# Twenty-three instead of twenty-one MLP pairs in block products, weights rounded by DMA, and a new planned order

## The chip, the cores and the metric

The kernel runs on 1 core of one Trainium2 chip. The metric is the device time of one execution in microseconds (us), lower is better. The inputs are float32, one batch of 256 tokens with 1024 features.

## The reference

Two decoder layers. Each has a token mixer (block-sparse attention in layer 0, dilated window attention in layer 1) and then an MLP; each half ends in a layer norm. What the change touches is the MLP, with `x` of 256 x 1024, `w_in` of 1024 x 4096 and `w_out` of 4096 x 1024:

```python
def sq_relu_mlp(x, w_in, w_out):
    return jnp.square(jax.nn.relu(x @ w_in)) @ w_out

for i in range(2):
    mix = moba_attention(h, ...) if i == 0 else dilated_attention(h, ...)
    h = layer_norm(ALPHA * h + mix, ...)
    h = layer_norm(ALPHA * h + sq_relu_mlp(h, w_in[i], w_out[i]), ...)
```

## The kernel before, in words

**Products in three terms.** A float32 operand is split into a high part, rounded to the matmul type `fp32r` (tile `whi` for weights), and a low part, the rest (`wlo`). A product is the sum of hi*hi, hi*lo and lo*hi, so one float32 product costs three matmuls on TensorE (PE). A weight tile is 128 x 1024, 512 KB. It is loaded by SP into a `raw` buffer (7 of them, `NRAW`), ScalarE (ACT) writes `whi` (10 buffers), and VectorE (DVE) subtracts and writes `wlo` (10 buffers); this is `split` (L406 to L414) called by `load_near`.

**The far path.** For the tiles named in `FAR` and `FAR_W`, DVE is spared: `far_parts` (L422) lets ACT write `whi` (L423) and minus `whi` into `wlo` (L424), and then GpSimd (POOL) issues a DMA that reads the weight tile from HBM a second time and adds it into `wlo` (L425). `FAR` names MLP tiles, one set for each layer: `("f", p, t)` is tile t of pair p in the first product, `("o", p, k)` and `("s", p, n)` are tiles of the second. `FAR_W` numbers the 58 other tiles (projections, and the head of each MLP) in program order.

**Pairs.** The 4096 hidden columns are 16 pairs p of 256. For pairs 2 to 15 the first product is `do_first` (L1207), a step `fpt` for each half t: 8 matmuls of 512 columns and 8 of 256. `half_sum` (L1124) then adds two halves of the PSUM bank, by an ACT copy and a DVE addition, and `square` (L1130) makes the squared ReLU, by two ACT instructions where `SQUARES` says `A`, by one DVE instruction where it says `D`. Pairs 0 and 1 come from `head` and `half` (L1158, L1164).

**Ordinary pairs and block products.** The second product of a pair is ordinary (`o` or `O`, `do_out`, L1236) or a block product (`a` or `A`, `do_duo`, L1249). An ordinary pair multiplies two weight tiles for two halves of the tokens: 24 matmuls of 512 columns. A block product treats pair and weights as 2 x 2 blocks and needs seven products instead of eight: 21 matmuls of 512 columns, 9 in its step `a`/`A` and 12 in its step `b`. For that DVE and ACT make more: `duo_sums` (L660) forms sums of the activation blocks (four subtractions or additions of 128 columns, and low parts of 512 and 384 columns), and `load_duo` (L677) loads two raw tiles, forms four sums of 512 columns of weights (two before the first step, two before the second) and splits half a tile and three whole ones. Where a pair is in `BY_DMA`, the first two of the four sums are made by one adding DMA from POOL (L698). `combine` (step `z`, L1281) adds the seven products up into the output tokens. Upper-case letters make the activation parts early, in cells of their own that `Cells` hands out, lower-case ones when needed.

**The order.** `STEPS` (L37) is the order of the work on PE in each MLP, written out: first products, block products and ordinary pairs are mixed so that weights and sums come in time. `Plan` (L145 on) holds every operation with a cost; `Plan.order` works out due times backwards from PE's order, lists every engine's operations in a simulated order, and emits them so; each engine then runs its list in order. `landed` (L113) is the planner's cost of a transfer. `GB_AT` and `MASK_AT` name the steps at which the layer-norm weights and the second attention mask are loaded. Around the step lists stand the attention stages and the layer norms, which the change does not reorder by hand.

**The end.** After `z` the last ordinary pairs run, for tokens 0 to 127 and then 128 to 255 (`out_and_ln`, L1090), while DVE does `combine` and the first layer norm; then comes the last layer norm (`ln_last`, L1022).

Of the kernel before, what the change touches and what calls it, by code (L numbers as in the profile page):

```python
# [347 lines left out]
def tile_trunk(  # L348
# [94 lines left out]
    def load_near(src, n=1024):
        w = W()
        w.raw = mk([P, 1024], F32, "raw", NRAW)
        w.hi = mk([P, 1024], F32R, "whi", NHI)
# [1 line left out]
        dma(lambda: w.raw.t[:, :n], src[:, :n], (), [(w.raw, 0)], P * n * 4)
        split(
            n, lambda: w.raw.t[:, :n], lambda: w.hi.t[:, :n], lambda: w.lo.t[:, :n],  # L450
            [(w.raw, 0)], [(w.hi, 0)], [(w.lo, 0)], sbuf=True,
        )
        return w

# [1173 lines left out]
```

## Time and profile before

| | |
|---|---|
| time, median of 3 runs | 546.07 us (546.03 to 546.39) |
| time of the profiled execution | 548.12 us |
| its span, first to last instruction | 546.3 us |
| mean granted TensorE clock | 0.996 |
| DMA from POOL (queue q0) | 37 issues, 19.40 MB |
| loads from HBM by SP (queue q1) | 104.35 MB |
| mean DMA rate | 229 GB/s |

The profile is one execution. Busy time of an engine is the time in which one of its instructions runs; instructions overlap a little, so the pitch from one start to the next is what an instruction really takes of a busy engine. Matmul ends are modelled, so PE is read by the starts too. In a row such as `L413 DVE TENSOR_TENSOR wlo<-raw,whi`, L413 is the line (here of a helper), `wlo<-raw,whi` what is written from what. A bracket `[1.06 <-DVE q0lo L749]` says how long the engine stood idle before, and what released it. Rows of the view by stretches hold, for each engine, its busy time and instructions, then the granted clock, the share of the 16 DMA engines and GB/s.

### The profile page before, as it was taken

What the parts mean: (1) busy time and instruction counts of PE and PEld (TensorE: products, weight loads), DVE (VectorE), ACT (ScalarE), POOL (GpSimd) and SP (SyncE); (2) the same over time, 40 slices, a digit from 0 to 9 for tenths busy, and PEclk for the clock granted to TensorE, in tenths of its full rate; (3) what the DMA queues carried; (4) which work ended last, traced back from release to release, by engine and by line L of the source; (5) the groups of instructions that cost most, each with busy time, mean ns of one, the idle gap of its engine ahead of it and who ended that gap; (6) DMA issues with size and microseconds to landing.
All of it is one profiled execution on the core that took longest, in us unless ns stands there. A gap on an engine that the chain in (4) does not pass through costs nothing.

```text
span 546.3 us, 8734 instructions
## 1 busy us (share of the span) xinstructions
PE 537.5 (98%) x3172; PEld 458.5 (84%) x3172; DVE 476.1 (87%) x846; ACT 389.8 (71%) x613; POOL 41.7 (8%) x52
## 2 busy tenths in 40 slices
PE   9999999999999999999999999999999999999994
PEld 7989888888888878888888889888888888888884
DVE  6679998897899899899857789879889899899997
ACT  6558999278799768798645558746876997877530
POOL 0000010010001000100011000110010100100001
PEclk9999999999999999999999999999999999999998
DMA  8987787929869879979998756865894989885602
GB/s 331 343 328 242 190 196 197 382 88 308 229 155 237 279 220 288 225 182 324 338 252 224 253 179 173 246 201 138 277 278 118 227 280 268 261 202 178 215 24 78
DMA packets 35611, 125.03 MB, mean 229 GB/s; under 512 B 3952, under 2 KB 4848, under 8 KB 35568
## 3 DMA queue, kind: packets, MB, share of 16 engines
q1 hardware_dynamic: 29664, 104.35, 55.9%
q0 software_dynamic: 5328, 19.40, 19.7%
q10 hardware_dynamic: 576, 0.72, 0.4%
q8 instruction: 25, 0.41, 0.3%
q14 instruction: 18, 0.15, 0.1%
HBM read 123.40 MB, written 1.05 MB: 228 GB/s over the span
## 4 chain that ended last, share of the span: by engine, by line
PE 94%; DVE 2%; DMA 2%; ACT 0%; issue 0%; POOL 0%; DVEq 0%; POOLq 0%; ACTq 0%
PE acc L417 59%; PE tp L417 32%; PE tp L890 3%; DMA raw<-in_win_dram 2%; DVE wlo L413 1%; ACT whi L408 0%; DVE raw L749 0%; POOL rstd L1004 0%; DVE tok L756 0%; DVEq L1622 0%; DVE ta L749 0%; DVE ta L413 0%; DVE pt L413 0%; DVE bst L1035 0%; ACT ta L1127 0%
## 5 line engine op out<-in xcount | busy, mean ns | idle before, releaser
L413 DVE TENSOR_TENSOR wlo<-raw,whi 128x1024 fp32r<-128x1024 f32 (+2 forms) x200 | 222.8, 1137 | 22.1 <-ACT whi L408 20.2
L408 ACT ACTIVATE whi<-raw 128x1024 fp32r<-128x1024 f32 (+2 forms) x198 | 191.0, 995 | 49.8 <-PE acc L417 14.4
L417 PE MATMUL acc<-xs,whi 128*128 128x512 f32 (+1 forms) x496 | 113.4, 374 | 1.1 <-DVE q0lo L749 1.1
L417 PEld LDWEIGHTS acc<-xs,whi 128*128 128x128 f32 x496 | 87.1, 191 | 17.8 <-DVE q0lo L749 1.5
L417 PEld LDWEIGHTS acc<-xs,wlo 128*128 128x128 f32 x448 | 60.0, 191 | 3.5 <-issue 0.2
L417 PE MATMUL acc<-xs,wlo 128*128 128x256 f32 x448 | 62.5, 283 | 0.0
L417 PE MATMUL tp<-xs,whi 128*128 128x512 f32 x224 | 56.3, 392 | 0.0
L417 PE MATMUL acc<-whi,ahi 128*128 128x512 f32 (+1 forms) x130 | 49.7, 392 | 0.0
L417 PEld LDWEIGHTS tp<-xs,whi 128*128 128x128 f32 x224 | 40.4, 189 | 7.3
L417 PE MATMUL acc<-wlo,ahi 128*128 128x512 f32 (+1 forms) x109 | 42.3, 388 | 0.0
L423 ACT ACTIVATE whi<-raw 128x1024 fp32r<-128x1024 f32 x28 | 29.5, 1053 | 16.4 <-PE acc L417 15.3
L417 PE MATMUL acc<-whi,alo 128*128 128x512 f32 (+1 forms) x108 | 39.3, 388 | 0.0
L417 PEld LDWEIGHTS tp<-xs,wlo 128*128 128x128 f32 x224 | 30.5, 190 | 2.1
L417 PE MATMUL tp<-xs,wlo 128*128 128x256 f32 x224 | 31.5, 283 | 0.0
L424 ACT ACTIVATE wlo<-whi 128x1024 fp32r<-128x1024 f32 x28 | 29.6, 1058 | 0.4
L417 PE MATMUL acc<-whi,xs 128*128 128x512 f32 (+1 forms) x112 | 29.0, 364 | 0.0
L417 PEld LDWEIGHTS acc<-whi,ahi 128*128 128x128 f32 x130 | 24.4, 188 | 5.0 <-issue 0.3
L749 DVE TENSOR_TENSOR ta<-acc,ta 128x256 f32<-128x256 f32 x41 | 17.0, 421 | 12.1 <-ACT ta L777 8.7
L417 PE MATMUL tp<-whi,xs 128*128 128x512 f32 x80 | 25.4, 396 | 0.0
L417 PE MATMUL acc<-whi,ta 128*128 128x512 f32 (+1 forms) x72 | 24.5, 384 | 0.0
L417 PEld LDWEIGHTS acc<-whi,alo 128*128 128x128 f32 x108 | 20.3, 188 | 4.2
L417 PEld LDWEIGHTS acc<-wlo,ahi 128*128 128x128 f32 x109 | 20.5, 188 | 3.8
(246 smaller groups left out, 947.8 us busy)
## 6 DMA issues: line engine op xcount, KB each, us to landing
raw<-in_win_dram SPq DMA_DIRECT2D x64, 512.0 KB, 5.7
raw<-in_wout_dram SPq DMA_DIRECT2D x64, 512.0 KB, 6.1
raw<-in_wqk_dram SPq DMA_DIRECT2D x22, 512.0 KB, 8.9
raw<-in_wo_dram SPq DMA_DIRECT2D x14, 512.0 KB, 5.3
wlo<-in_win_dram POOLq DMA_DIRECT2D x10, 512.0 KB, 9.2
raw<-in_wout_dram POOLq DMA_DIRECT2D x9, 512.0 KB, 8.5
raw<-in_wv_dram SPq DMA_DIRECT2D x8, 512.0 KB, 5.4
wlo<-in_wqk_dram POOLq DMA_DIRECT2D x7, 512.0 KB, 9.2
```

The costliest lines, as they stand in the source:

```text
L408: op("ACT", act(n, sbuf=sbuf), lambda: nc.scalar.activation(hi(), src(), AF.Copy), r, whi)
L413: lambda: nc.vector.tensor_tensor(lo(), src(), f32(hi()), op=ALU.subtract), list(r) + list(whi), wlo,
L417: nc.tensor.matmul(out_ap, lhsT, rhs, start=start, stop=stop)
L423: op("ACT", act(1024, sbuf=True), lambda: nc.scalar.activation(hi.t, raw.t, AF.Copy), keys, [(hi, 0)])
L424: op("ACT", act(1024, sbuf=True), lambda: nc.scalar.activation(lo.t, f32(hi.t), AF.Copy, scale=-1.0), [(hi, 0)], [(lo, 0)])
L749: op("DVE", dve(n) + extra, lambda: nc.vector.tensor_tensor(out_ap(), a(), b(), op=alu), r, w)
L890: nc.tensor.transpose(ps.t[:, c : c + P], src(), ident.t)
```

## The change

- `STEPS` is new. Layer 0 has 11 block products and 5 ordinary pairs instead of 10 and 6, layer 1 has 12 and 4 instead of 11 and 5. As before, 2 ordinary pairs of layer 0 and 3 of layer 1 come after `z`.
- `M` is a new kind of block product: its activation parts lie in the buffer of the attention mask (`m1`) while that is free. (`G`, the same in the buffers of the layer-norm weights, and the undivided first chunk, `whole`, are in the code and not used by these lists.) The mask for layer 1 is loaded at step `b9` instead of `f21`, the layer-norm weights at `fb1` instead of `fc1`.
- `CAST` and `CAST_W` name 12, 11 and 21 tiles, 44 in all, whose `whi` is written by a DMA from POOL that rounds on the way from HBM (`cast_in`), instead of by ACT. Where the tile is not `FAR` as well, SP still loads the raw tile for DVE's low part; where it is both, no raw tile is loaded.
- `FAR` and `FAR_W` name 11, 13 and 7 tiles (31) instead of 8, 6 and 14 (28). 15 of the 31 are also rounded by DMA. Three of them, `("s", 5, 1)`, `("s", 5, 2)` and `("s", 10, 2)`, are weight sums: the adding DMA reads them from their buffer and not from HBM.
- `BY_DMA` keeps one pair of nine (pair 6 of layer 1). `TWICE` would make the second two sums by DMA too, but only for pairs in `BY_DMA`, and it does not name pair 6 of layer 1; so that branch is not taken.
- `SQUARES` gives 3 pairs of layer 0 and 4 of layer 1 to DVE.
- The planner takes buffers of a tag in turn instead of the one free first, and has new costs for a DMA that adds (8.8 instead of 8.4) or rounds (7.0).

The diff, cut to its core:

```diff
 STEPS = (
-    "f20 fd0 f21 f30 fc0 f40 f31 f41 fa0 fd1 f80 fa1 f90 A4 f50 f81 f51 Aa Ad fc1 ba f70 bd b4 A2 fb0 f91 "
-    "b2 ac fe0 f71 fe1 A3 f60 bc ff0 f61 b3 ff1 Ae fb1 A6 a7 be b6 A8 o1 b7 b8 ob o0 o9 z O5 Of",
-    "f20 f21 fd0 f30 fc0 f40 fd1 f41 fa0 f80 f31 f81 f50 fa1 f51 Ad f90 Aa A4 fc1 ba f70 b4 f71 bd A2 b2 "
-    "f91 ac fe0 fe1 fb0 f60 A3 bc ff0 b3 ff1 f61 A5 fb1 Ae a7 b5 be A6 O9 o1 b7 Ab b6 bb z Of o0 o8",
+    "f30 fc0 f31 fc1 f50 fa0 fa1 f80 f81 f20 f51 f40 A3 f21 fd0 fe0 b3 M2 fb0 fb1 f41 fd1 b2 A8 f90 b8 "
+    "fe1 Ac f91 f70 ff0 ff1 Ab f60 f61 bc bb A9 A5 f71 b9 b5 Aa ba a4 b4 Af O6 a7 b7 bf oe o0 z o1 Od",
+    "fd0 f40 f80 fd1 fc0 f81 f41 f50 f30 f51 fc1 A4 f70 f71 fb0 fb1 f31 A8 fe0 Ac fa0 b4 bc fe1 f20 f90 "
+    "A3 fa1 b3 b8 Ad f21 Mb f91 bd Aa bb ff0 ff1 ba f60 f61 A7 b7 Af o1 bf A5 a6 M2 b5 b2 b6 z Oe o0 O9",
 )
-BY_DMA = ({2, 6, 8, 14}, {2, 5, 6, 10, 14})
+BY_DMA = (set(), {6})
 FAR = (
-    {("f", 7, 0), ("f", 10, 1), ("f", 12, 0), ("f", 12, 1), ("f", 14, 1), ("o", 1, 1), ("s", 6, 0), ("s", 10, 0)},
-    {("f", 2, 1), ("f", 7, 0), ("f", 11, 0), ("f", 14, 1), ("s", 10, 0), ("s", 14, 0)},
+    {("f", 2, 1), ("f", 4, 0), ("f", 6, 0), ("f", 11, 1), ("f", 13, 1), ("f", 15, 1), ("o", 1, 0), ("s", 5, 1), ("s", 5, 2), ("s", 7, 0), ("s", 9, 0)},
+    {("f", 2, 0), ("f", 3, 1), ("f", 10, 0), ("f", 13, 0), ("f", 13, 1), ("f", 14, 0), ("o", 1, 0), ("o", 1, 1), ("s", 6, 0), ("s", 8, 0), ("s", 10, 0), ("s", 10, 2), ("s", 11, 0)},
 )
-FAR_W = {0, 12, 14, 16, 21, 32, 34, 35, 36, 39, 43, 48, 53, 57}
-GB_AT, MASK_AT = "fc1", "f21"
-SQUARES = ("AAAAAAAAAAAAAAAA", "AAAAAAAAAAAAAAAA")
+FAR_W = {10, 26, 34, 42, 51, 53, 56}
+GB_AT, MASK_AT = "fb1", "b9"
+CAST = (
+    {("f", 2, 1), ("f", 3, 0), ("f", 3, 1), ("f", 4, 0), ("f", 4, 1), ("f", 12, 0), ("f", 13, 1), ("o", 0, 1), ("o", 1, 0), ("o", 13, 0), ("o", 14, 1), ("s", 15, 0)},
+    {("f", 2, 0), ("f", 4, 0), ("f", 8, 0), ("f", 10, 0), ("f", 13, 0), ("f", 13, 1), ("f", 14, 0), ("o", 0, 1), ("o", 1, 0), ("o", 1, 1), ("s", 11, 0)},
+)
+CAST_W = {0, 4, 7, 10, 11, 15, 16, 18, 19, 21, 22, 29, 36, 38, 39, 43, 45, 50, 51, 53, 54}
+TWICE = ({2, 3, 9, 10, 11, 12, 15}, {8, 10, 11, 12, 13})
+SQUARES = ("AAAAADAAAAAADAAD", "AAAADDAAAADAAADA")
 def kinds_of(i):
-    at = {int(x[1], 16): x[0] for x in STEPS[i].split() if x[0] in "oOaA"}
-    return ["sS"["aA".index(at[p])] if at[p] in "aA" else at[p] for p in range(DFF // 256)]
+    at = {int(x[1], 16): x[0] for x in STEPS[i].split() if x[0] in "oOaAGM"}
+    return [at[p].replace("a", "s").replace("A", "S") for p in range(DFF // 256)]
...
         bus = max(t + DMA_FETCH, bus) + o.xfer / 370e3
-        return bus, max(bus, t + DMA_LANDS)
+        return bus, max(bus, t + (DMA_CASTS if o.xfer % 2 else DMA_LANDS))
     t = max(t + FETCH, bus)
     t += o.xfer / next(rate for until, rate in RATES if t < until)
...
-                s = max(s, sorted(slots[tag])[len(bs) - 1])
+                s = max([s] + slots[tag][: len(bs)])
...
                 if not b.held:
-                    slots[b.tag].remove(min(slots[b.tag]))
...
-DMA_ISSUE, DMA_FETCH, DMA_LANDS, DMA_RING = 1.0, 2.0, 8.4, 6
+DMA_ISSUE, DMA_FETCH, DMA_LANDS, DMA_CASTS, DMA_RING = 1.0, 2.0, 8.8, 7.0, 6
...
-    def far_parts(raw, hi, lo, src, keys):
-        op("ACT", act(1024, sbuf=True), lambda: nc.scalar.activation(hi.t, raw.t, AF.Copy), keys, [(hi, 0)])
+    def cast_in(hi, src):
+        op("POOL", DMA_ISSUE, lambda: nc.gpsimd.dma_start(hi.t, src), (), [(hi, 0)], xfer=P * 1024 * 4 - 1)
+    def add_in(lo, hi, src, keys=()):
         op("ACT", act(1024, sbuf=True), lambda: nc.scalar.activation(lo.t, f32(hi.t), AF.Copy, scale=-1.0), [(hi, 0)], [(lo, 0)])
-        op("POOL", DMA_ISSUE, lambda: nc.gpsimd.dma_start(lo.t, src, accum_op=ALU.add), (), [(lo, 0)], xfer=P * 1024 * 8)
-    def load_far(src):
+        op("POOL", DMA_ISSUE, lambda: nc.gpsimd.dma_start(lo.t, src(), accum_op=ALU.add), keys, [(lo, 0)], xfer=P * 1024 * 8)
+    loads = [0]
+    def load_w(src):
+        loads[0] += 1
+        return load_as(src, loads[0] - 1 in FAR_W, loads[0] - 1 in CAST_W)
+    def load_as(src, far, cast):
         w = W()
-        w.raw = mk([P, 1024], F32, "raw", NRAW)
+        if not (far and cast):
+            w.raw = mk([P, 1024], F32, "raw", NRAW)
         w.hi = mk([P, 1024], F32R, "whi", NHI)
         w.lo = mk([P, 1024], F32R, "wlo", NLO)
-        dma(lambda: w.raw.t, src, (), [(w.raw, 0)], P * 1024 * 4)
-        far_parts(w.raw, w.hi, w.lo, src, [(w.raw, 0)])
+        if not (far and cast):
+            dma(lambda: w.raw.t, src, (), [(w.raw, 0)], P * 1024 * 4)
+        if cast:
+            cast_in(w.hi, src)
+        else:
+            op("ACT", act(1024, sbuf=True), lambda: nc.scalar.activation(w.hi.t, w.raw.t, AF.Copy), [(w.raw, 0)], [(w.hi, 0)])
+        if far:
+            add_in(w.lo, w.hi, lambda: src)
+        else:
+            low_part(w.raw, w.hi, w.lo, [(w.raw, 0)])
         return w
...
+        def spot(self, tag):
+            if tag in self.gone:
+                raise ValueError(tag)
+            b = mk([P, 1024], F32R, tag, 1)
+            return [(b, 0, 0), (b, 512, 1)]
...
-        def wide(t, src=None):
+        def wide(t, part, src, again):
             h, l = [mk([P, 1024], F32R, tag, n) for tag, n in (("whi", NHI), ("wlo", NLO))]
-            if src is not None:
-                far_parts(t, h, l, src, [(t, 0), (t, 1)])
-                return [(h, l, c, 0) for c in (0, 512)]
-            split(1024, lambda: t.t, lambda: h.t, lambda: l.t, [(t, 0), (t, 1)], [(h, 0)], [(l, 0)], sbuf=True)
+            keys = [(t, 0), (t, 1)]
+            if part in cast:
+                cast_in(h, src)
+            else:
+                op("ACT", act(1024, sbuf=True), lambda: nc.scalar.activation(h.t, t.t, AF.Copy), keys, [(h, 0)])
+            if part in far:
+                add_in(l, h, again, [] if src is not None else keys)
+            else:
+                low_part(t, h, l, keys)
             return [(h, l, c, 0) for c in (0, 512)]
         split(512, x0, part(hi, q * 512, 512), part(lo, q * 512, 512), xk[:1], [(hi, q)], [(lo, q)], sbuf=True)
-        w3, w2 = wide(y, pair[:, 1024:] if far else None)
+        w3, w2 = wide(y, 0, pair[:, 1024:], lambda: pair[:, 1024:])
         if by_dma:
             op(
                 "POOL", DMA_ISSUE, lambda: nc.gpsimd.dma_start(x.t, pair[:, 512:1536], accum_op=ALU.add), xk, xk,
             tt(512, x0, x0, x1, ALU.add, xk, xk[:1])
             tt(512, x1, x1, y0, ALU.add, xk[1:] + yk[:1], xk[1:])
         yield w2, w3, (hi, lo, q * 512, q)
-        w5, w7 = wide(x)
-        tt(512, y0, y0, x0, ALU.add, yk[:1] + xk[:1], yk[:1])
-        tt(512, y1, y1, y0, ALU.add, yk, yk[1:])
-        w6, w4 = wide(y)
+        w5, w7 = wide(x, 1, None, lambda: x.t)
+        if by_dma > 1:
+            op(
+                "POOL", DMA_ISSUE, lambda: nc.gpsimd.dma_start(y1(), pair[:, :512], accum_op=ALU.add), yk[1:], yk[1:],
+                xfer=P * 512 * 8,
+            )
+            op("POOL", DMA_ISSUE, lambda: nc.gpsimd.dma_start(y.t, x.t, accum_op=ALU.add), xk + yk, yk, xfer=P * 1024 * 8)
+        else:
+            tt(512, y0, y0, x0, ALU.add, yk[:1] + xk[:1], yk[:1])
+            tt(512, y1, y1, y0, ALU.add, yk, yk[1:])
+        w6, w4 = wide(y, 2, None, lambda: y.t)
...
+                    n = {"O": 2, "S": 4, "M": 2}.get(kinds[p], 0)
+                    u = cells.take(F32) if kinds[p] in "os" else (mk([P, 512], F32, "ta", NTA), 0, 0)
+                    homes = [h for tag in {"G": ("g", "b"), "M": ("m1",)}.get(kinds[p], ()) for h in cells.spot(tag)]
+                    homes += [cells.take(F32R, True) for _ in range(n)]
...
-                weights = load_duo(wout[i][p], (*single[0], q), p in BY_DMA[i], ("s", p, 0) in FAR[i])
+                weights = load_duo(wout[i][p], (*single[0], q), (p in BY_DMA[i]) * (1 + (p in TWICE[i])), *[
+                    {n for n in range(3) if ("s", p, n) in parts[i]} for parts in (FAR, CAST)
+                ])
...
```

More of the change, by code (lines that the diff above doesn't have):

```diff
@@ L440, in load_w, with low_part @@
         loads[0] += 1
-        return (load_far if loads[0] - 1 in FAR_W else load_near)(src)
-    def load_near(src, n=1024):
+        return load_as(src, loads[0] - 1 in FAR_W, loads[0] - 1 in CAST_W)
+    def load_as(src, far, cast):
         w = W()
-        w.raw = mk([P, 1024], F32, "raw", NRAW)
+        if not (far and cast):
+            w.raw = mk([P, 1024], F32, "raw", NRAW)
         w.hi = mk([P, 1024], F32R, "whi", NHI)
         w.lo = mk([P, 1024], F32R, "wlo", NLO)
[L448 to L452, printed above, removed]
-        return w
+        if not (far and cast):
[8 more added lines that the diff above has]
+            low_part(w.raw, w.hi, w.lo, [(w.raw, 0)])
+        return w
+    def low_part(raw, hi, lo, keys):
+        tt(1024, lambda: lo.t, lambda: raw.t, lambda: f32(hi.t), ALU.subtract, [*keys, (hi, 0)], [(lo, 0)])
     xs = [mk([P, 4, 2, S], F32R, f"xs{i}", 1) for i in range(2)]
@@ L675, in duo_sums, with load_duo @@
         return b11, b12, b22, q1, q2, q3, q4
-    def load_duo(pair, single, by_dma, far):
+    def load_duo(pair, single, by_dma, far, cast):
         x, y = [mk([P, 1024], F32, "raw", NRAW) for _ in range(2)]
@@ L1146, in relu_sq_tok @@
         t = slice(m * P, (m + 1) * P)
+        quads = lambda tile: tile.rearrange("p (j s) -> p j s", j=4)
+        if alo is None:
+            op(
+                "ACT", act(512), lambda: nc.scalar.activation(quads(ahi.t)[:, :, t], quads(pt.t), AF.Copy), [pt],
+                [(ahi, j) for j in range(4)],
+            )
+            return
         keys = [(j, m) for j in range(4)]
         split(
-            512, lambda: pt.t.rearrange("p (j s) -> p j s", j=4), lambda: ahi.t[:, :, t], lambda: alo.t[:, :, t],
+            512, lambda: quads(pt.t), lambda: ahi.t[:, :, t], lambda: alo.t[:, :, t],
             [pt], [(ahi, k) for k in keys], [(alo, k) for k in keys],
@@ L1160, in head @@
             self.ws = [[load_w(win[i][c * 4 + j]) for j in range(4)] for c in range(nx)]
-            self.chunks = {c: act_tiles() for c in range(nx)}
+            whole = kinds_of(i)[0] in "sS"
+            self.chunks = {c: (mk([P, 1024], F32, "ahi", 3), None) if whole else act_tiles() for c in range(nx)}
             self.half(0)
@@ L1183, in rest @@
             prods = []
-            nduo = sum(k in "sS" for k in kinds)
+            nduo = sum(k in "sSGM" for k in kinds)
             single = [None]
@@ L1204, in load @@
             def load(src, key):
-                return (load_far if key in FAR[i] else load_near)(src)
+                return load_as(src, key in FAR[i], key in CAST[i])
             def do_first(p, t):
@@ L1211, in do_first @@
                 if t == 0:
-                    n = {"O": 2, "S": 4}.get(kinds[p], 0)
-                    u = cells.take(F32) if not n else (mk([P, 512], F32, "ta", NTA), 0, 0)
-                    homes = [cells.take(F32R, True) for _ in range(n)]
+                    n = {"O": 2, "S": 4, "M": 2}.get(kinds[p], 0)
+                    u = cells.take(F32) if kinds[p] in "os" else (mk([P, 512], F32, "ta", NTA), 0, 0)
+                    homes = [h for tag in {"G": ("g", "b"), "M": ("m1",)}.get(kinds[p], ()) for h in cells.spot(tag)]
+                    homes += [cells.take(F32R, True) for _ in range(n)]
                     taken[p] = homes or [u]
@@ L1295, in combine @@
                 tt(512, lambda: z1.t[:, hi], w(p5), lambda: z1.t[:, hi], ALU.add, [(z1, 1), p5], [(z1, 1)])
+            if chunks[0][1] is None:
+                for p in range(2 * nx):
+                    homes = [cells.take(F32R, True) for _ in range(4)] if kinds[p] == "S" else []
+                    held[p] = (chunks[0][0], p * 512, 2 * p), homes
+                    taken[p] = homes
+                    if homes:
+                        ready(p)
             late_ = False
@@ L1309, in rest @@
                     do_out(c, late_)
-                elif step[0] in "aA":
+                elif step[0] in "aAGM":
                     duos[c] = do_duo(c)
```

33 lines of the change are left out of this document (18 added, 15 removed).

## The prediction

> **What bounds the kernel now.** I read the page's busy times and chain, PE's waits, its starts, then the stretches of the two MLPs.
>
> ```profile
> PE 537.5 (98%) x3172; PEld 458.5 (84%) x3172; DVE 476.1 (87%) x846; ACT 389.8 (71%) x613; POOL 41.7 (8%) x52
> PE 94%; DVE 2%; DMA 2%; ACT 0%; issue 0%; POOL 0%; DVEq 0%; POOLq 0%; ACTq 0%
> ...
> PE acc L417 <- DVE q0lo L749: 1.1, 1, 1.1
> PE tp L417 <- PEq L1613: 0.8, 1, 0.8
> ```
>
> PE carries 94% of the chain and has one wait for data in the whole run, 1.1 us; the other is its start. Busy PE could still hide lost time, so I look at starts:
>
> ```profile
> 127.69 34.47 PE tp L417 x200
> ...
> 257.93 27.20 PE acc L417 x120
> ...
> 383.21 39.80 PE tp L417 x230
> ```
>
> 120 matmuls of 512 columns take 27.20 us, 0.2267 each. Layer 0's step list begins at 127.69, layer 1's at 383.21. This stretch gives the pitch of 256 columns, and the one wait:
>
> ```profile
> 191.56 2.95 DVE L413 TENSOR_TENSOR wlo<-raw,whi 128x512 fp32r<-128x512 f32 x3
> 193.46 0.39 PE L417 MATMUL tp<-whi,alo 128*128 128x512 f32 x1
> 194.43 0.42 DVE L749 TENSOR_TENSOR q0lo<-acc,q0lo 128x256 f32<-128x256 f32 x1
> 194.90 2.11 PE L417 MATMUL acc<-xs,whi 128*128 128x512 f32 x8 [1.06 <-DVE q0lo L749]
> 196.85 1.11 PE L417 MATMUL acc<-xs,wlo 128*128 128x256 f32 x8
> 197.81 0.40 PE L417 MATMUL tp<-whi,alo 128*128 128x512 f32 x1
> ```
>
> Eight take 197.81 - 196.85 = 0.96 us; a step `f` is 8 x 0.2267 + 0.96 = 2.77 us. Layer 1's list before has 28 such steps (77.6), 11 block products of 21 matmuls (52.4) and 5 ordinary pairs of 24 (27.2): 157 us, and 383.21 + 157 = 540.2 is where PE ends within a microsecond. So PE runs through the list without gaps; layer 0 has the one gap, where a half-sum on DVE stood behind three low parts. PE's work sets the time. DVE is close behind:
>
> ```profile
> 127.00:285.00 158.00, 156.94 (x798) 133.38 (x797) 139.55 (x213) 123.88 (x173) 13.14 (x15) 1.00 0.87 257
> 383.00:540.00 157.00, 156.30 (x810) 133.86 (x808) 146.00 (x229) 112.35 (x163) 9.61 (x11) 1.00 0.70 205
> 490.00:522.00 32.00, 32.00 (x147) 26.64 (x146) 30.48 (x45) 22.23 (x29) 0.00 (x0) 1.00 0.60 182
> ...
> 200.00:230.00 30.00, 30.00 (x160) 25.77 (x159) 27.05 (x37) 22.69 (x34) 2.61 (x3) 1.00 0.94 245
> ```
>
> In layer 1's list DVE is busy 146.0 of 157 us; from 490 to 522 95%, and PE still waits for nothing.
>
> **PE's part of the change.** Two ordinary pairs become block products: 2 x (24 - 21) = 6 matmuls fewer, 6 x 0.2267 = 1.36 us. All else on PE, the late pairs after `z` too, keeps its number of instructions. The Trainium skill's page "TensorE: Matmul & The Clock Gate", section "Wait — 56ns, not 53.3ns?", gives 215.7 ns for this pitch at full clock; the sum by it would be 1.29 us. The measured pitch decides. The gap of 1.06 us belongs to the old order; the new one may lose it, but has DVE fuller and may have another: I take half, 0.5 us.
>
> **DVE's part.** A row's duration overlaps its neighbour, so I cost by pitch:
>
> ```profile
> 162.15 0.28 DVE L749 TENSOR_TENSOR ta<-ta 128x128 f32<-128x128 f32 x1
> 162.35 0.28 DVE L749 TENSOR_TENSOR ta<-ta,ta 128x128 f32<-128x128 f32 x1
> ...
> 165.13 0.55 DVE L413 TENSOR_TENSOR sc<-ta,sc 128x384 fp32r<-128x384 f32 x1
> 165.60 2.35 DVE L413 TENSOR_TENSOR wlo<-raw,whi 128x1024 fp32r<-128x1024 f32 x2
> ...
> 515.14 0.69 DVE L749 TENSOR_TENSOR raw<-raw 128x512 f32<-128x512 f32 x1
> 515.75 8.17 DVE L413 TENSOR_TENSOR wlo<-raw,whi 128x1024 fp32r<-128x1024 f32 x7
> 523.84 0.68 DVE L413 TENSOR_TENSOR ta<-sc,ta 128x512 fp32r<-128x512 f32 x1
> ```
>
> 128 columns: 0.20 us; 384: 0.47; 512: 0.61; 1024: (523.84 - 515.75) / 7 = 1.16. In each layer 12 more weight sums of 512 columns fall to DVE (layer 0: from 32 to 44, as 4 of 10 block products had two by DMA and now none of 11 has; layer 1: from 34 to 46): 12 x 0.61 = 7.3. One more `duo_sums` is 4 x 0.20 + 0.61 + 0.47 = 1.9 (half a weight tile more makes up for an ordinary pair's split). Whole low parts: layer 0 has 70 tiles less 8 far, then 71 less 11, 2 fewer, -2.3; layer 1 has 71 less 6, then 72 less 13, 6 fewer, -7.0. The squares, one instruction of 512 columns each: 3 x 0.61 = 1.8 and 4 x 0.61 = 2.4. Net: +8.7 us in layer 0, +4.7 us (with roundings) in layer 1. Outside the lists 7 fewer far tiles are +8.1 us of DVE, over some 230 us. DVE's idle time covers it: 158 - 139.55 = 18.5 us and 157 - 146.0 = 11.0 us. Then layer 0 has 148.3 busy of 156.3, layer 1 150.7: 96%, with 5.6 us left for all its waits. Those waits now:
>
> ```profile
> DVE wlo L413 <- ACT whi L408: 3.2, 5, 1.3
> DVE ta L749 <- ACT ta L1127: 2.1, 8, 0.5
> DVE ta L749 <- ACT ta L1136: 1.8, 4, 0.9
> DVE ahi L413 <- ACT ahi L408: 1.2, 2, 0.9
> ```
>
> All four (layer 1's list, 8.3 us of the 11) are waits for ACT, and ACT gets lighter; the third falls away for the pairs that DVE squares itself. DVE can run dense: seven low parts end to end, 8.17 us of weights, were made ahead of PE.
>
> **ACT, POOL and the DMA engines.**
>
> ```profile
> L408 ACT ACTIVATE whi<-raw 128x1024 fp32r<-128x1024 f32 x171 | 175.9, 1056 | 47.4 <-PE acc L417 14.4 <-PE tp L417 11.1 <-DVE raw L749 11.1
> ...
> q1 hardware_dynamic: 29664, 104.35, 55.9%
> q0 software_dynamic: 5328, 19.40, 19.7%
> ...
> raw<-in_win_dram SPq DMA_DIRECT2D x64, 512.0 KB, 5.7
> ...
> wlo<-in_win_dram POOLq DMA_DIRECT2D x10, 512.0 KB, 9.2
> ...
> L698 POOL DMA_DIRECT2D raw<-in_wout_dram x9: 862/862/889, 174.9 to 488.8; - x9
> ```
>
> ACT's whole-tile instructions, high parts and far tiles' negatives together, go from 78 to 70 in layer 0, 77 to 74 in layer 1 and 72 to 44 outside: 39 x 1.06 = 41 us less of 390, none of it on the path. POOL issues 76 DMAs (44 + 31 + 1) instead of 37, at 0.86 us each 34 us more, on an engine that is 8% busy; but a DMA that waits for its buffer holds up the layer norms' powers (`rstd`) behind it. No row shows that; I cost it at nothing, at most one issue (0.86 us) for each of the four MLP norm halves.
>
> A plain 512 KB load takes 0.559 x 546.3 / 199 = 1.53 us of all 16 DMA engines (104.35 MB are 199 such tiles), an adding one 0.197 x 546.3 / 37 = 107.6 / 37 = 2.91. No row shows a rounding DMA. It moves the bytes of a plain load and reads no target, so I take 1.53, with 2.91 as the other end. Layer 0: 12 roundings, one adding DMA fewer (12 before, 11 now), 4 raw loads fewer: +9.4 us, at the other end +25.9. Layer 1: 11 roundings, 3 adding more, 7 loads fewer: +14.8, or +30.0. Outside: 21 roundings, 7 adding and 3 loads fewer: +7, or +36 in 230 us. Shares become (0.87 x 158 + 9.4) / 156.3 = 0.94 in layer 0 and 0.80 in layer 1; the stretch from 200 to 230 had 0.94 with no wait on PE. A rounded high part lands 5.7 to 9.2 us after its issue by the two landing rows, against ACT's 1.06, and DVE's low part waits for it; early issue into 10 `whi` buffers covers that. Where it doesn't, the low part stands at the head of DVE's list, behind it the half-sums that free banks for PE: what the one gap shows.
>
> **The moved pieces.** SP's list loses 14 raw loads (tiles that are both rounded and added by POOL), and the mask and table for layer 1 pass from step `f21` to `b9`, 105 us into layer 0's list (adding up PE's steps), so about 233; the layer-norm weights stay near 50 and 41 us into the lists. All are used after the lists end (layer 0's at 127.69 + 157 = 284.7), so I cost the moves at nothing; SP's queue without cover would delay a raw load by two such transfers, 2 x 1.53 us. In layer 1 pairs 2 and b share the mask's buffer: pair 2's parts, summed after `f21`, must wait until PE has read pair b's in `bb`, five steps after; PE wants them in `M2`, 33 us behind `bb`, which hides it.
>
> **Sum.** 546.07 - 1.36 - 0.5 = 544.2. The profiled execution ran 548.12 with a span of 546.3; in its terms 546.2 and a span of 544.4.
>
> **The rivals.**
> 1. *DVE takes over (slower).* In layer 1 the busy 150.7 us stay with the 11.0 us of waits: 161.7 instead of 157. With layer 0's gain (0.68 + 0.5) that is 546.07 + 4.7 - 1.2 = 549.6. It decides from 6 us of waits on. For it: adding DVE's pitches along the lists, the longest run of steps in which DVE's work exceeds PE's time was `a7 be b6` (11.9 against 7.5) in layer 0 and `A3` to the first `be` (34.7 against 30.1) in layer 1, and becomes `bc` to `bf` (49.2 against 42.2) and `A3` to `bb` (33.2 against 27.3). Excesses of 4.5 and 4.6 us become 7.0 and 5.9, against 8.17 us of lead seen. Against it: ACT's relief, and the dense rows.
> 2. *The gain is eaten by new waits of one to three us (same),* where excesses of 7.0 and 5.9 meet a lead of 5 to 6: 545.0 to 547.1.
> 3. *The DMA engines run full (slower).* With 2.91 per rounding, layer 0 needs 0.87 x 158 + 25.9 = 163.4 us of engines in 156.3: 7.1 late, 546.07 - 1.36 + 7.1 = 551.8. Against it: the bytes. The Trainium skill's page "DMA: Bandwidth & Descriptors", section "Queues, rings and completion order", says that a DMA engine takes turns between queues, packet by packet; by that, roundings slow every raw load beside them. No run here shows it yet.
>
> That the change does not do what it says holds for `TWICE` alone, which nothing calls; PE's count doesn't hang on it.
>
> **How the numbers follow.** A difference of 0.2%, 1.1 us, is about what a measurement of this kernel can tell. Forecast (PE stays the bound, 543.5 to 544.9): 0.55. Rival 2: 0.22. Rival 1: 0.17, rival 3: 0.06, both slower, 0.23. Low end: both PE terms in full, 546.07 - 1.36 - 1.06 = 543.65, less 0.3 for small gaps between stages, 543.3. High end 549.6, rival 1 in full; rival 3's 0.06 is left out. The forecast's own range is 543.3 to 545.
>
> **What would show it.** Right: 3166 matmuls, one PE wait for data at most, DVE at 95% and more in both lists with waits for ACT whi shrunk, ACT near 345 us, queue q0 near 107.6 - 5 x 2.91 + 44 x 1.53 = 160 us of engines. Wrong: several waits of PE for `wlo`, `whi` or a half-sum (rival 1), rounding DMAs that cost nearer 2.9 us and raw loads that land far later than 5.7 us (rival 3), or a last layer norm that starts late because DVE trails PE at the end.

## The result, and the profile after

The changed kernel takes 552.81 us (median of 4 runs, 551.87 to 553.11), the kernel before 546.09 us (546.03 to 546.39, 4 runs): a ratio of 1.0119, 95% interval 1.0102 to 1.0137. It is 6.7 us slower, above the high end of the forecast range. The profiled execution of the changed kernel took 551.87 us, its span is 550.0 us.

The page's lines of busy times and of the chain:

```profile
PE 537.8 (98%) x3166; PEld 458.2 (83%) x3166; DVE 496.4 (90%) x888; ACT 348.2 (63%) x564; POOL 61.4 (11%) x91
PE 91%; DMA 5%; DVE 1%; issue 1%; SPq 0%; POOL 0%; ACT 0%; DVEq 0%; POOLq 0%; ACTq 0%
```

PE has the 6 matmuls fewer (3166) and ACT is at 348, both as forecast. New is the 5% of DMA in the chain, from 2%. To see where the time went I cut the span at four points of the chain of waits that both kernels have: the first matmul of layer 0's list, the seam to layer 1's attention, the first matmul of layer 1's list, and the last ordinary pair. The kernel before was profiled a second time for this, unchanged (below, `before_again`), since its first profile held a gap that the second one does not have. The view by stretches, the second profile of before:

```profile
127.02:283.94 156.92, 156.92 (x801) 134.01 (x800) 140.40 (x214) 124.18 (x174) 13.14 (x15) 1.00 0.88 258
381.14:528.94 147.80, 147.80 (x757) 126.14 (x756) 138.12 (x212) 112.12 (x162) 8.68 (x10) 1.00 0.72 214
```

and the changed kernel:

```profile
133.28:289.87 156.59, 156.45 (x797) 133.40 (x797) 149.15 (x233) 115.79 (x162) 17.54 (x24) 1.00 0.85 265
387.17:534.21 147.04, 147.04 (x753) 125.57 (x753) 142.83 (x228) 108.20 (x156) 14.20 (x19) 1.00 0.79 235
```

| part | before, us | changed, us | difference |
|---|---|---|---|
| up to layer 0's list | 127.02 | 133.28 | +6.26 |
| layer 0's list | 156.92 | 156.59 | -0.33 |
| layer 1's attention | 97.20 | 97.30 | +0.10 |
| layer 1's list | 147.80 | 147.04 | -0.76 |
| end (spans 544.4 and 550.0) | 15.46 | 15.79 | +0.33 |

The lists, where the block products are, gained 1.09 us. Nearly all the loss lies before layer 0's list, which holds no step list and no block product. The page's longest waits of PE and PEld (the weight load) in the changed kernel, and PE's starts there:

```profile
PEld acc L423 <- ACT whi L453: 3.1, 1, 3.1
PE acc L423 <- DVE ta L779: 2.7, 1, 2.7
```

```profile
21.23 1.70 PE L423 MATMUL acc<-xs,whi 128*128 128x256 f32 x12 [1.03 <-ACT whi L414]
...
23.49 2.00 PE L423 MATMUL acc<-xs,whi 128*128 128x512 f32 x8
28.20 3.27 PE L423 MATMUL acc<-xs,whi 128*128 128x512 f32 x8 [2.71 <-DVE ta L779]
31.27 2.47 PE L423 MATMUL acc<-xs,wlo 128*128 128x256 f32 x16
33.57 2.00 PE L423 MATMUL tp<-whi,xs 128*128 128x512 f32 x8
```

In the second profile of before the first of these 512-column matmuls starts like this, and PE then runs on:

```profile
21.75 3.82 PE L417 MATMUL acc<-xs,whi 128*128 128x512 f32 x16
```

The loss by the starts: 23.49 - 21.75 = 1.74 us up to there; then 28.20 - 23.49 - 8 x 0.2267 = 2.90; then eight matmuls take 31.27 - 28.20 = 3.07 us instead of 1.81, 1.26 more; and sixteen of 256 columns take 33.57 - 31.27 = 2.30 instead of 16 x 0.12 = 1.92, 0.38 more. Together 6.28, the whole loss. The last two terms are no waits; the stretches say what they are, in the column before the share: the granted clock falls.

```profile
25.00:30.00 5.00, 2.29 (x9) 1.53 (x8) 4.37 (x7) 1.65 (x2) 0.00 (x0) 0.88 1.04 418
30.00:35.00 5.00, 5.00 (x27) 4.45 (x26) 5.00 (x7) 3.71 (x6) 0.00 (x0) 0.78 1.03 419
```

Both stands go back to loads of SP that land late. Ahead of the first (1.03 us) these are the start loads of the activations (`raw`, `g`, `b`, `tok`, 512 KB each from `in_xw`), which ACT rounds as they land. ACT's timeline, first the second profile of before, then the changed kernel:

```profile
9.81 0.42 ACT L408 ACTIVATE xs<-g 128x256 fp32r<-128x256 f32 x1
11.14 0.42 ACT L408 ACTIVATE xs<-b 128x256 fp32r<-128x256 f32 x1 [0.17 <-DMA b<-in_xw_dram]
12.38 0.42 ACT L408 ACTIVATE xs<-tok 128x256 fp32r<-128x256 f32 x1
13.62 0.42 ACT L408 ACTIVATE xs<-tok 128x256 fp32r<-128x256 f32 x1
```

```profile
11.43 0.42 ACT L414 ACTIVATE xs<-g 128x256 fp32r<-128x256 f32 x1 [1.75 <-DMA g<-in_xw_dram]
14.01 0.42 ACT L414 ACTIVATE xs<-b 128x256 fp32r<-128x256 f32 x1 [1.43 <-DMA b<-in_xw_dram]
16.58 0.42 ACT L414 ACTIVATE xs<-tok 128x256 fp32r<-128x256 f32 x1 [1.41 <-DMA tok<-in_xw_dram]
20.03 0.42 ACT L414 ACTIVATE xs<-tok 128x256 fp32r<-128x256 f32 x1 [2.30 <-DMA tok<-in_xw_dram]
```

Before, a tile comes every 1.24 us (12.38 to 13.62); after, every 2.57 us (14.01 to 16.58) and more: half the rate, and the last one 6.41 us late. The longer stand (2.71 us) hangs on what SP's queue carries behind these loads, the first tiles of weights. Pieces of the chain of the changed kernel (start, duration):

```profile
7.04 16.10 DMA raw<-in_wqk_dram
...
23.23 1.24 DVE wlo L779
...
24.54 1.07 ACT whi L453
...
26.77 1.29 DVE ta L779 x2
...
28.20 5.54 PE acc L423 x24
```

The tile is under way for 16.10 us. Only then follow DVE's low part, ACT's first high part of a whole weight tile (at 24.54 us; at 15.54 in the second profile of before), another low part, and `ta`, which stands behind the low parts in DVE's list and ends PE's stand.

What shares the DMA engines with all these loads stands on POOL's timeline:

```profile
4.15 0.73 POOL L429 DMA_DIRECT2D whi<-in_wqk_dram  x1
4.88 0.54 POOL L429 DMA_DIRECT2D whi<-in_wv_dram  x1
6.53 0.53 POOL L429 DMA_DIRECT2D whi<-in_wqk_dram  x1 [1.10 <-DVE xs L419]
10.72 0.53 POOL L429 DMA_DIRECT2D whi<-in_wqk_dram  x1 [3.67 <-DVE wlo L419]
15.04 0.53 POOL L429 DMA_DIRECT2D whi<-in_wqk_dram  x1 [3.79 <-DVE xs L419]
```

These are the five first tiles of `CAST_W` (0, 4, 7, 10, 11): POOL has nothing else to do at the start and issues the rounding DMAs as soon as their buffers allow. In the kernel before no DMA of POOL is issued ahead of 18.01 us. And there was no room for them: in the kernel before, too, the DMA engines were full from 5 to 35 us, for instance in these two of the six rows of 5 us (first profile; all six show 1.01 to 1.04):

```profile
10.00:15.00 5.00, 5.00 (x44) 5.00 (x44) 5.00 (x9) 4.53 (x8) 0.00 (x0) 1.00 1.03 419
...
30.00:35.00 5.00, 5.00 (x26) 4.26 (x25) 3.10 (x5) 0.60 (x1) 0.00 (x0) 1.00 1.03 419
```

The Trainium skill's page "DMA: Bandwidth & Descriptors", section "Queues, rings and completion order", says that a DMA engine with work from several queues serves them in turn, packet by packet. The trace agrees: with one queue beside it, SP's queue gets half (2.57 us for a tile instead of 1.24).

### The profile page after: what moved, and what is told of

The parts are those of the page before. It is cut to its first block, busy times and chain, and to the rows that moved or that the text cites. A ratio compares the mean times of both kernels' runs of the same rounds, so it can differ in the third digit from the quotient of the medians.

```text
span 550.0 us, 8781 instructions
## 1 busy us (share of the span) xinstructions
PE 537.8 (98%) x3166; PEld 458.2 (83%) x3166; DVE 496.4 (90%) x888; ACT 348.2 (63%) x564; POOL 61.4 (11%) x91
## 3 DMA queue, kind: packets, MB, share of 16 engines
q1 hardware_dynamic: 27648, 97.01, 49.5%
## 4 chain that ended last, share of the span: by engine, by line
PE 91%; DMA 5%; DVE 1%; issue 1%; SPq 0%; POOL 0%; ACT 0%; DVEq 0%; POOLq 0%; ACTq 0%
PE acc L423 57%; PE tp L423 31%; DMA raw<-in_wqk_dram 3%; PE tp L920 3%; DMA wlo<-in_wout_dram 2%; DVE wlo L779 1%; DMA raw<-in_xw_dram 1%; SPq L410 0%; DVE tok L786 0%; POOL rstd L1034 0%; DVE ta L779 0%; ACT whi L453 0%; DVEq L1673 0%; DVE bst L1065 0%; DVE mv L1032 0%
## 5 line engine op out<-in xcount | busy, mean ns | idle before, releaser
L779 DVE TENSOR_TENSOR wlo<-raw,whi 128x1024 fp32r<-128x1024 f32 x170 | 201.9, 1219 | 4.7 <-ACT whi L453 3.2
L423 PE MATMUL acc<-xs,whi 128*128 128x512 f32 (+1 forms) x536 | 124.6, 376 | 3.9 <-DVE ta L779 2.7
L453 ACT ACTIVATE whi<-raw 128x1024 fp32r<-128x1024 f32 x90 | 93.4, 1056 | 38.8 <-PE acc L423 15.3
L423 PEld LDWEIGHTS acc<-xs,whi 128*128 128x128 f32 x536 | 94.4, 190 | 22.4 <-ACT whi L453 3.1
L710 ACT ACTIVATE whi<-raw 128x1024 fp32r<-128x1024 f32 x67 | 69.6, 1053 | 14.9 <-DVE raw L779 9.0
L423 PE MATMUL tp<-xs,whi 128*128 128x512 f32 x184 | 46.3, 392 | 0.0
L423 PEld LDWEIGHTS tp<-xs,whi 128*128 128x128 f32 x184 | 33.2, 189 | 6.0
L779 DVE TENSOR_TENSOR raw<-raw,raw 128x512 f32<-128x512 f32 x45 | 30.9, 688 | 0.8
L779 DVE TENSOR_TENSOR raw<-raw 128x512 f32<-128x512 f32 x45 | 30.8, 686 | 0.4
L433 POOL DMA_DIRECT2D wlo<-in_win_dram x14 | 12.2, 872 | 145.1 <-ACT wlo L432 99.2
L414 ACT ACTIVATE xs<-tp 128x512 fp32r<-128x512 f32 x12 | 6.7, 595 | 33.5 <-PE tp L920 33.4
```

What stands on the lines that cost most here:

```text
L414: op("ACT", act(n, sbuf=sbuf), lambda: nc.scalar.activation(hi(), src(), AF.Copy), r, whi)
L423: nc.tensor.matmul(out_ap, lhsT, rhs, start=start, stop=stop)
L433: op("POOL", DMA_ISSUE, lambda: nc.gpsimd.dma_start(lo.t, src(), accum_op=ALU.add), keys, [(lo, 0)], xfer=P * 1024 * 8)
L779: op("DVE", dve(n) + extra, lambda: nc.vector.tensor_tensor(out_ap(), a(), b(), op=alu), r, w)
```

## The experiments

**Theory.** The five early roundings take DMA time when the engines are full, and PE, which hangs on the start loads, pays. **Rivals:** rounding DMAs are dear by themselves, wherever they are; the planner's new rule and costs order the work worse; DVE, which is fuller, takes over; the profile of before was not typical.

**Without the five (`noearly`).**

```diff
-CAST_W = {0, 4, 7, 10, 11, 15, 16, 18, ...}
+CAST_W = {15, 16, 18, ...}
```

> The changed kernel, with tiles 0, 4, 7, 10 and 11 of the list of other tiles no longer rounded by DMA (ACT writes their high parts); all else, step lists, planner and the other 39 roundings, as in the changed kernel. Theory, early roundings: the five DMAs that POOL issues at 4.15, 4.88, 6.53, 10.72 and 15.04 us take DMA time from the loads of the start, PE waits there and loses about 6 us, and the two MLP lists gain what was forecast. It expects 543.5 to 545.5 us, no wait of PE between 16 and 30 us, and the last start load landed by about 14 us. Rival, new order: the planner's rule for buffers and the new step lists cost the time; it expects 551 to 553.

546.56 us (545.74 to 547.21, 11 runs), ratio to before 1.0 (0.9991 to 1.0008). 552.81 - 546.56 = 6.2 us come back, and the second group of scores of layer 0's attention on PE (`tp<-q0hi`) starts at 53.23 instead of 58.78. The other 39 roundings stay in, so they are not what costs 6 us. But the time is a microsecond above what was expected, and the kernel only equals the one before: the block products' gain is not in it. Its stretches:

```profile
127.70:284.05 156.35, 156.35 (x798) 133.40 (x797) 149.16 (x233) 115.67 (x163) 17.60 (x24) 1.00 0.86 264
381.36:529.20 147.84, 147.47 (x754) 125.44 (x753) 142.89 (x228) 108.41 (x156) 14.36 (x19) 1.00 0.79 232
```

Layer 0 has 0.57 us of its 0.68. Layer 1 has nothing (147.84 against 147.80): PE stands there once, for an adding DMA whose source is a sum that DVE makes (`("s", 10, 2)`), 483.89 - 483.13 - 0.2267 = 0.53 us late by the starts:

```profile
483.13 0.39 PE L423 MATMUL tp<-whi,v 128*128 128x512 f32 x1
483.89 0.50 PE L423 MATMUL tp<-wlo,v 128*128 128x512 f32 x1 [0.37 <-DMA wlo<-raw]
```

**Only two of the five (`two`).** `CAST_W` with 0 and 4 of the five.

> The changed kernel with two of the five early roundings (tiles 0 and 4) and not 7, 10 and 11. Early roundings, priced by bytes: the DMA engines are full until 35 us, so each 512 KB there costs about 1.25 us; two of five give 546.5 + 2.5 = 549 us. If only one of them does the harm, it is either 546.5 or 552.5.

547.43 us (546.88 to 547.81, 10 runs), ratio 1.0009 (1.0 to 1.0018): 0.9 us above `noearly` by the medians, 0.5 by the ratios, where a fifth of 6.2 us for each would be 2.5: a miss for the price by bytes. PE has one start gap of 0.53 us, and its second group of scores starts at 53.65, 0.42 us later than in `noearly`. A reading that fits is that PE has a lead over the loads which swallows most of the first two. The other three then cost 5 to 6 us together; they were not tried one by one.

**Held behind the start loads (`hold`).** All 44 roundings, but POOL first reads a column of the last start load, and the five take what it writes as an input:

```diff
+        if n == 0:
+            last = stages[-1].raw
+            op("POOL", 0.1, lambda: nc.gpsimd.tensor_copy(warm.t[:, 1:2], last.t[:, S : S + 1]), [(last, 1)], [(warm, 1)])
+        return load_as(src, n in FAR_W, n in CAST_W, [(warm, 1)] if n < 12 else ())
```

> The changed kernel with all its 44 roundings, but a copy of one element on POOL, which reads the last start load, stands ahead of the five early ones, so they are issued only when that load has landed. Early roundings: most of the loss goes, 544 to 547 us; what is left would be the wait for high parts that land 7 us after about 14 us. New order: 551 to 553. A third reading, that a rounding harms wherever it stands, expects 551 or more as well.

552.12 us (550.14 to 553.77, 5 runs), ratio 1.0092 (1.0075 to 1.011): a miss for the theory in its first form. ACT rounds the last start load at 15.54 us (13.62 before, 20.03 changed), and PE does not stand for it; the five are issued from 16.43 us on, and PE waits later, for a high part of the projections:

```profile
36.42 3.60 PE L423 MATMUL acc<-xs,whi 128*128 128x512 f32 x8 [4.81 <-ACT whi L457]
```

The chain goes back from there to a raw tile of weights that SP issues at 20.65 us and that is under way for 14.59 us; the DMA share is 1.04 to 1.09 from 20 to 40 us. So it is not enough to let the start loads go first: the weights behind them are needed as urgently. The theory is mended to that: what these kernels add to full engines at the start is paid, once PE's lead is used up. That a rounding harms wherever it stands, which also expected 551 or more, is ruled out by the 39 in `noearly`.

**The same bytes without rounding (`plain_five`).** The kernel before, and ten plain DMAs of 128 x 512 from POOL at the start, into buffers not yet in use: the bytes of five tiles, which nothing reads. Seven of the ten are issued from 4.31 us on; the last three come only at 24.84 us, behind an adding DMA in POOL's list.

```diff
+    for i, (tag, n) in enumerate([("sc1", 4)] * 4 + [("v", 4)] * 4 + [("pt0", 2)] * 2):
+        b = mk([P, 512], F32, tag, n)
+        src = wo0[i // 2][:, i % 2 * 512 : i % 2 * 512 + 512]
+        op("POOL", DMA_ISSUE, lambda b=b, src=src: nc.gpsimd.dma_start(b.t, src), [(stages[HELD].raw, 0)], [b], xfer=P * 512 * 4)
```

> The kernel before, with ten plain DMAs of 128 x 512 float32 (the bytes of five tiles) issued by POOL right after its first copy at about 4 us, into buffers that nothing uses yet; their data is overwritten unread. If early roundings cost because they are transfers beside the start loads, plain ones cost the same: 550 to 553 us. If it is the rounding, or the wait for rounded parts, these cost little: 546 to 547.5.

559.71 us (558.85 to 560.67, 4 runs), ratio 1.024 (1.0226 to 1.0255), more than expected. PE's starts:

```profile
21.17 1.69 PE L417 MATMUL acc<-xs,whi 128*128 128x256 f32 x12 [1.15 <-ACT whi L408]
...
27.51 2.08 PE L417 MATMUL acc<-xs,whi 128*128 128x512 f32 x8 [2.09 <-DVE ta L753]
...
31.96 1.19 PE L417 MATMUL tp<-whi,xs 128*128 128x512 f32 x4 [1.42 <-ACT whi L408]
```

The same two places wait as in the changed kernel, and a third, and the second group of scores is at 58.73, nearly as there (58.78; before: 52.52). Plain bytes do such damage too, so the rounding is not needed for it; that the two times agree so closely is luck, since only seven of the ten were issued early and PE waits at one place more. The other 7 us of this kernel come later, in an order that the planner made anew around the added DMAs; one such place is below under the hardware.

**The five in the old order (`oldtables_five`), and the old tables in the new code (`oldtables`).** The changed code with the tables and step lists of before: once with `CAST_W = {0, 4, 7, 10, 11}` and once with none.

> The changed kernel's code with the step lists and all tables of the kernel before (21 block products, old far tiles, no squares on DVE), and only tiles 0, 4, 7, 10 and 11 rounded by DMA. Early roundings: 546.1 plus 5 to 7, so 551 to 553 us, with the same waits of PE between 16 and 30 us. New step lists as the cause: 545 to 547.

> The changed kernel's code and planner rules (buffers in turn, new costs of DMAs) with all tables and step lists of the kernel before, no roundings. New order as a cause: 548 or more. Early roundings as the only cause: 546 to 547, as before.

With the five: 557.0 us (556.61 to 557.9, 4 runs), ratio 1.0193 (1.0179 to 1.0207), more than expected and at another place: PE has no long wait between 16 and 30 us, but one of 6.83 us at 38.94, for ACT's high part. In this order POOL issues one of the five at 4.42 us and the other four only from 19.66 us on, behind an adding DMA; the chain goes back to a raw tile of weights that is under way for 16.72 us, as in `hold`. Without: 546.37 us (545.97 to 547.12, 10 runs), ratio 0.9998 (0.9989 to 1.0007). So the five alone cost 10.6 us in the old order, and the planner's rule and costs without them cost nothing.

**The kernel before again (`before_again`).** Unchanged.

> The kernel before, unchanged, for a profile on the chip of these comparisons. Its first profile came from an execution of 548.12 us, 2 us above the median of its timed runs. If the one gap of PE at 193.46 us (1.06 us and a cold start of matmuls behind it) belongs to the kernel, it is there again and the span is near 546; if it belonged to that execution, the gap is gone, the span is near 544.5, and the forecast's term for it (0.5 us) was never to be had.

546.38 us (546.06 to 547.95, 10 runs); its profiled execution took 546.19 us with a span of 544.4, and PE has no gap near 193 us. The 1.06 us gap that I quoted belonged to one execution, 2 us above the usual one.

**The changed lists with the old start (`oldfront`).** `FAR_W` of before and no `CAST_W`; the lists and their roundings as changed.

> The changed kernel with the far tiles outside the MLP lists as before and no roundings there (none of the 21); MLP lists, roundings in them, block products and planner as changed. If the start alone held the gain back, this is the forecast's part in isolation: 1.36 us less than before, 544.5 to 545.3. If the new lists cost something of their own, 546 to 547 as with the five early roundings taken out.

547.53 us (546.16 to 548.72, 11 runs), ratio 1.0019 (1.0009 to 1.0029): a miss. Here PE stands 1.14 us for the same adding DMA at 485.25. But the run changes more than the start: all 21 roundings outside the lists are gone and the old far tiles are back, in layer 1's attention as well. From the end of layer 0's last ordinary pairs (the transposes behind them, at 288.37) to layer 1's list it takes 93.71 us, against 91.97 in `before_again`. It shows that the old start does not bring the gain by itself; it does not isolate the lists.

**The lists without their roundings (`nomlpcast`).** `noearly` with `CAST` empty.

> The changed kernel without the five early roundings and without the 23 of the MLP lists (the other 16 stay): ACT writes those high parts, some 24 us more of ACT. If PE is the bound in the lists whatever ACT does there, the time is that of the kernel without the five, 546 to 547. If the roundings carry the two more block products, waits of PE for weights come up in the lists: 548 to 552.

553.0 us (552.81 to 553.16, 4 runs), ratio 1.0115 (1.0102 to 1.0129). PE waits for low parts in five places, the longest (1.6 us) for an adding DMA, and the end runs over DVE, for the last layer norm:

```profile
538.91 2.02 DVE tok L783 x3
...
543.72 0.99 DVE bst L1059 x3
```

The 23 roundings in the lists carry the block products: without them the kernel is 553.0 - 546.56 = 6.4 us slower. This is how rival 1 of the prediction looks, waits for low parts and an end on DVE, once ACT's work is put back.

**Is one adding DMA what ate layer 1's gain?** `noearly` with far tiles changed. First away with the one that PE waited for (`noearly_near`), then with two in layer 0 as well (`noearly_nosum`):

```diff
-    {..., ("s", 8, 0), ("s", 10, 0), ("s", 10, 2), ("s", 11, 0)},
+    {..., ("s", 8, 0), ("s", 10, 0), ("s", 11, 0)},
```

and in `noearly_nosum` this as well:

```diff
-    {..., ("o", 1, 0), ("s", 5, 1), ("s", 5, 2), ("s", 7, 0), ("s", 9, 0)},
+    {..., ("o", 1, 0), ("s", 7, 0), ("s", 9, 0)},
```

> The changed kernel without the five early roundings and with one far tile fewer: the low part of the last weight sum of pair 10 in layer 1 is DVE's again, not an adding DMA's. Without the five, the one wait left to PE in the lists stood there (0.37 us at 483.9, matmuls slowed behind it; 1.14 us with the older far tiles outside). If that wait eats the forecast's gain, the time falls by 0.5 to 1 us, to 545.5 to 546.0. If DVE, 1.16 us fuller, trails at the end, it stays at 546.5 or rises.

> As the run with one far tile fewer, and also the two weight sums of pair 5 in layer 0 split by DVE, so that no adding DMA reads a sum from its buffer. DVE has 2.3 us more in layer 0. If DVE still has room there, the same time as that run within 0.5 us; if layer 0 is at DVE's limit, one to two us more.

547.53 us (546.7 to 548.26, 11 runs), ratio 1.0012 (1.0003 to 1.0021), and 551.4 us (549.9 to 552.46, 4 runs), ratio 1.007 (1.005 to 1.0091). The wait at 484 us is gone in the first, but its low part is now DVE's, 1.16 us more, and the chain ends on DVE: `tok` and the statistics `bst` of the last layer norm (here `noearly_near`) end after PE.

```profile
536.91 0.99 DVE bst L1062 x3
537.90 0.05 DVE bst L1045
537.95 0.38 DVE bst L1065
```

In the second, PE waits in layer 0 for DVE's low parts and, at 276.35, 2.21 us for an adding DMA. Two low parts more, 2.3 us of DVE, are more than layer 0's order can take; how much of the loss is DVE's and how much the DMA's was not separated.

Then the far tile was moved and not removed: `("s", 10, 2)` replaced by `("f", 15, 0)`, `("f", 6, 0)` or `("f", 9, 1)`, tiles whose adding DMA waits for no sum:

```diff
-    {("f", 2, 0), ..., ("s", 10, 0), ("s", 10, 2), ("s", 11, 0)},
+    {("f", 2, 0), ("f", 15, 0), ..., ("s", 10, 0), ("s", 11, 0)},
```

> The changed kernel without its five early roundings, and in layer 1 the far tile ("s", 10, 2) replaced by ("f", 15, 0): the same number of adding DMAs and of DVE low parts, but no adding DMA that must wait for a sum on DVE. Theory A, the gain of the block products was eaten in layer 1 by that one waiting DMA (0.53 us of PE at 483.9): layer 1's list becomes about 0.6 us shorter than the kernel before's and the time 545.5 to 546.0, ratio about 0.999. Theory B, DVE has no slack in layer 1, and any other placing moves the wait: PE waits for a low part or DVE trails at the end, time 546.4 to 547.5.

> The same with ("f", 6, 0), the step right behind the one that waited, as the far tile in place of ("s", 10, 2). Theory A: 545.5 to 546.0. Theory B: 546.4 to 547.5, and another place for the wait than with ("f", 15, 0).

> The same with ("f", 9, 1), two steps ahead of the one that waited, as the far tile. Theory A: 545.5 to 546.0. Theory B: 546.4 to 547.5.

546.9 us (545.66 to 548.13, 11 runs; ratio 1.0005, 0.9995 to 1.0014), 547.9 us (547.64 to 548.47, 8 runs; 1.0024, 1.0014 to 1.0034) and 546.48 us (546.01 to 547.99, 11 runs; 1.0001, 0.9992 to 1.001). None is faster. The wait moves, as theory B has it (the second costs even more than it said). With `("f", 15, 0)` PE now stands here:

```profile
509.85 0.50 PE L423 MATMUL acc<-wlo,ta 128*128 128x512 f32 x1 [0.65 <-DMA wlo<-in_wout_dram]
```

with `("f", 6, 0)` here:

```profile
505.81 0.50 PE L423 MATMUL acc<-wlo,ahi 128*128 128x512 f32 x1 [1.21 <-DMA wlo<-in_wout_dram]
```

and with `("f", 9, 1)` the chain ends on DVE, as in `noearly_near`:

```profile
536.27 0.99 DVE bst L1062 x3
537.26 0.05 DVE bst L1045
```

No kernel of this study beats the one before.

## Why the prediction was wrong, point by point

- **The failed step** is in the part on ACT, POOL and the DMA engines: "Outside: 21 roundings, 7 adding and 3 loads fewer: +7, or +36 in 230 us". The sum was spread evenly over 230 us and found harmless. Five of the 21 fall in the first 15 us, where the engines have no room. The shares were read for the two lists only; the six rows from 5 to 35 us, with 1.01 to 1.04 in each, would have shown it. One rounding takes 0.175 x 40 us / 5 = 1.4 us of all engines there (row below, the queues of the changed kernel up to 40 us), so the five bring 7.0 us, less 1.24 for the one raw load that tile 10 no longer needs. Against `noearly` the second group of scores is 58.78 - 53.23 = 5.55 us later. The half clock adds 1.26 + 0.38 us to what the loads cost (PE's rows), and PE's lead seems to take some off (`two`); no run separates these parts.

```profile
q0 software_dynamic: 720, 2.62, 17.5%
```

- **Rival 3** (the DMA engines run full, 551.8) had half the mechanism, in the wrong place: layer 0's share is 0.85, not above 1, and a rounding is no dearer than a plain load. That its time is near the measured 552.81 is luck. Its sentence from the Trainium skill, that roundings slow the raw loads beside them, is what happened, at the start.
- **The price of a rounding** was right: 1.53 taken, 2.91 as the other end. By the queues of the whole page, q0 takes 0.288 x 550.0 = 158.4 us (forecast 160); less 32 adding DMAs, if each still takes 2.91, leaves 65.3 us for 44 roundings, 1.48 each. A plain load takes 0.495 x 550.0 / 185 = 1.47 there (97.01 MB are 185 tiles).

```profile
q1 hardware_dynamic: 27648, 97.01, 49.5%
q0 software_dynamic: 10944, 39.85, 28.8%
```

- **PE's 1.36 us** were right as work. 1.09 us appear in the lists of the changed kernel's profile (-0.33 and -0.76); in layer 0 a stand of PE at 278 us, 0.29 us, is what is missing but for 0.06. In the other kernels with these lists only layer 0's part is there: that list takes 156.15 us in `two`, `noearly_near` and `swap150`, against 156.92. Layer 1's list, 147.80 us before, takes 147.84 in `noearly`, 147.90 in `two`, 148.28 in `hold` and 148.50 in `swap150`: the 0.76 us there are one profile's.
- **The 0.5 us for the gap** was wrong: no such gap is in the usual execution (`before_again`). A stall seen once in one profile is no term of a sum.
- **DVE's part** was right to a tenth: by the two pairs of stretches, 149.15 - 140.40 = 8.75 us (forecast 8.7) and 142.83 - 138.12 = 4.71 (4.7). DVE is 95% and 97% busy in them, and PE runs on: rival 1 did not come in this kernel. It stands right behind, though: `nomlpcast`, `noearly_near` and `noearly_nosum` give it one to three low parts of 1.16 us more, or ACT its high parts back, and are 0.7 to 6 us slower than the kernel before by their ratios.
- **ACT, 41 us less**: 389.8 - 348.2 = 41.6. **POOL**: 39 instructions more as counted, but 19.7 us, not 34, since a rounding's issue takes 0.53 to 0.73 us.
- **The shares** forecast for the lists were 0.94 and 0.80; measured 0.85 and 0.79. Why layer 0 is lower stays open.
- **The moved pieces at nothing**: no wait of PE in the lists or behind them comes from the mask, the table or the layer-norm weights.
- **Rival 2** is what is left when the five roundings are taken out: in `noearly` PE's saved 1.36 us are met by 0.53 us for the adding DMA, and the time is that of before. What eats the remainder is only partly shown: in its profile the start is 0.7 us later than in `before_again` (127.70 against 127.02), but the start of `noearly_near`, with the same tables there, is not (127.03), and its time is no better, since DVE ends late. The timed runs of one kernel spread over 1.5 us, so a remainder of half a microsecond stays open.

## What to carry to other kernels

Transfers are not free because an engine issues them that has time: read the share of the DMA engines stretch by stretch, above all at the start, before a load is added or moved there. A change made for one stage must be followed through every place where its tables reach; here the lists gained 1.1 us at most and five entries for another stage lost 6.3. When PE, DVE and the adding DMAs are each within 1 or 2 us of the end of a list, work taken off PE only shows if the other two can give way as well.

## What the runs showed of the hardware

- A DMA that rounds from float32 to `fp32r` takes of the 16 engines what a plain load of its bytes takes (1.48 against 1.47 us for 512 KB in the changed kernel), about half of an adding one (2.91 in the kernel before). The 1.48 is an estimate by the queues; the start gives 1.4. POOL issues it in 0.53 to 0.73 us instead of 0.86.
- The granted clock fell after PE had stood for only 2.71 us, with 1.03 us a little earlier, and in `noearly_nosum` after 2.21 us (matmuls of 512 columns every 0.43 us from 277.41 on). It did not fall after 2.09 us in `plain_five` (eight matmuls from 27.51 to 29.43, 0.24 us each). Later in `plain_five` it fell after 2.99 us, and matmuls of 512 columns then came every 0.43 us for at least the next 4 us:

```profile
108.55 0.80 PE L417 MATMUL acc<-wlo,ahi 128*128 128x512 f32 x1 [2.99 <-DMA wlo<-in_wo_dram]
109.15 0.63 PE L417 MATMUL acc<-whi,alo 128*128 128x512 f32 x1
109.58 0.63 PE L417 MATMUL acc<-whi,ahi 128*128 128x512 f32 x1
```

The Trainium skill's page "TensorE: Matmul & The Clock Gate", section "What's actually happening", has the clock at half after an idle window of about 3.4 us, and its section "Wait — 56ns, not 53.3ns?" gives 426.7 ns for this pitch at half clock. The trace agrees with the pitch (109.58 - 109.15 = 0.43); the stands after which it fell were shorter here. So PE's wait of 2.71 us cost more than itself, 1.26 us more in the next eight matmuls.
